# Gated one-hots with the tokens innermost, read with a step by TensorE, and one form for all bank copies

## The chip, the core and the metric

The kernel runs on one core of a Trainium2 chip. The metric is the device time of one execution in microseconds (us), lower is better. Times of a kernel are given as the median of several runs; one further execution is taken by the hardware profiler, and every row of the profile is of that one. Engines are named as in the profile: PE is TensorE's matrix product and PEld its weight load, DVE is VectorE, ACT is ScalarE, POOL is GpSimd, SP is SyncE, which issues most of the transfers.

## The reference

Two transformer blocks in float32 over 256 tokens of width 1024. The change lies in the last part of the second block, a layer of 16384 experts: each token picks, for each of 8 heads, 16 experts by two keys of 128, and each pick has a gate (a softmax over the 16).

```python
def peer_ffn(h, w_query, sub_keys, u_emb, v_emb):
    ...
        q = (hc @ w_query).reshape(B, T_CHUNK, PEER_HEADS, 2, PEER_DKEY // 2)
        s = jnp.einsum('bthpd,hpnd->bthpn', q, sub_keys).astype(jnp.float32)
        s_top, i_top = lax.top_k(s, PEER_TOPK)
        ...
        g_s, pos = lax.top_k(cand, PEER_TOPK)
        e_idx = jnp.take_along_axis(cand_idx, pos, axis=-1)
        g = jax.nn.softmax(g_s, axis=-1)
        u = u_emb[e_idx]
        act = jax.nn.gelu(jnp.einsum('btd,bthkd->bthk', hc, u).astype(jnp.float32), approximate=False)
        return jnp.einsum('bthk,bthkd->btd', (g * act).astype(h.dtype), v_emb[e_idx])
```

The kernel gathers nothing. It computes the activation of every token with every expert, multiplies it by a gate that is zero where the token has not picked the expert, and multiplies the product by all of `v`. For this it needs, for each token, a matrix of 128 x 128 gates: entry (p, i) is the gate of the expert with first key i and second key p.

## The kernel before

`peer` does the layer. It first routes: queries, scores, the top 16 of each head and their gates. Beside that, and long after it, runs a loop over 64 chunks of 256 experts. `first(c)` splits a chunk of `u` into two fp32r parts (ScalarE at L172 writes `hi`, VectorE at L173 writes `lo`), makes 48 matmuls into the tile `pa` (L179 to L181), and ScalarE takes the gelu at L1355. The activations of the first 48 chunks (`BANK`) go to memory and come back; `second(c)` multiplies a chunk by its gates (L1372) and by `v`.

While the chunks 19 to 47 are on TensorE, `gates` makes the 256 gate matrices in between: it is a generator, and the loop takes a step of it every now and then (`done < 33 * (c + 1 - START) // (BANK - START)`), so that on TensorE the products of one batch of 8 tokens stand between the matmuls of two chunks. A step first has `hots` make the next batch's one-hots on VectorE:

- L1293: `x`, tile `hot`, bf16, laid out [key, token] with the 8 tokens innermost: 1 where the token's slot has that first key. Slots are on the partitions.
- L1294: `y`, tile `m`, float32, laid out [token, key]: the same for the second key.
- L1295: `z`, tile `hotg`, float32, laid out [token, key]: `x` times the slot's gate. Here `x` is read across its layout, so that two elements read after each other lie 8 bf16 apart.

Then TensorE makes, for each token, one float32 product of `y` (stationary) and `z` (moving, 128 columns) at L1309, four tokens to a PSUM bank (tile `acc`, four buffers), and ScalarE copies each bank into the tile `k` (`out` in the code), whose layout is [key, token of 16]. The two banks of a batch are copied in different forms. The copy of the second bank, at L1313, walks key by key and writes four neighbouring floats at a time, reading PSUM 128 floats apart. That of the first, at L1315, walks token by token: it reads PSUM in a row and writes floats that lie 16 apart. After two batches SyncE writes the 16 tokens' gates to memory (L1317).

Buffers: `hot` has 2, `hotg` 3, the tile `m` of `y` 3, `acc` 4 and `pa` 2. Nothing is scheduled by a planner; each engine's queue keeps the order in which the code is written.

Of the kernel before, what the change touches and what calls it, by code (L numbers as in the profile page):

```python
# [11 lines left out]
BF16 = mybir.dt.bfloat16  # L12
# [3 lines left out]
OP = mybir.AluOpType  # L16
# [3 lines left out]
P = 128  # L20
# [50 lines left out]
class Net:  # L71
# [1199 lines left out]
    def gates(self, slots, iotas, gd):  # L1271


        nc = self.nc
        keys, gate = [], []
        for t in range(2):
            pt = self.ps([P, 3, P], "acc", 4)
            for i in range(3):
                nc.tensor.transpose(pt[:, i, :], slots[t][:, i, :, :].rearrange("p a b -> p (a b)"), self.ident)
            kt = self.work([P, P], "key0", 2, BF16), self.work([P, P], "key1", 2)  # L1280
            gt = self.work([P, P], "gate", 2)
            for z, i in ((kt[0], 0), (kt[1], 1), (gt, 2)):
                nc.scalar.copy(z, pt[:, i, :])
            keys.append(kt)
            gate.append(gt)
        n = 8
        made = {}

        def hots(b):
            t, o = divmod(n * b, P)  # L1290
            wide = lambda x: x[:, o : o + n].unsqueeze(2).to_broadcast([P, n, P])
            x, y, z = self.work([P, P, n], "hot", 2, BF16), self.m4([P, n, P]), self.work([P, n, P], "hotg", 3)
            nc.vector.tensor_tensor(x, iotas[1], keys[t][0][:, o : o + n].unsqueeze(1).to_broadcast([P, P, n]), op=OP.is_equal)  # L1293
            nc.vector.tensor_tensor(y, iotas[0].unsqueeze(1).to_broadcast([P, n, P]), wide(keys[t][1]), op=OP.is_equal)  # L1294
            nc.vector.tensor_tensor(z, x.rearrange("p k t -> p t k"), wide(gate[t]), op=OP.mult)  # L1295
            made[b] = y, z

        hots(0)
        yield
        for b in range(32):  # L1300
            if b < 31:
                hots(b + 1)
            if b % 2 == 0:
                out = self.keep([P, P, 16], "k8", 4)
            y, z = made.pop(b)
            for q in range(0, n, 4):
                pg = self.ps([P, 4, P], "acc", 4)
                for i in range(4):
                    nc.tensor.matmul(pg[:, i, :], y[:, q + i, :], z[:, q + i, :], start=True, stop=True)  # L1309
                r = n * (b % 2) + q  # L1310
                o = out[:, :, r : r + 4]
                if q:
                    nc.scalar.copy(o, pg.rearrange("p t i -> p i t"))  # L1313
                else:
                    nc.scalar.copy(o.rearrange("p i t -> p t i"), pg)  # L1315
            if b % 2:
                nc.sync.dma_start(gd[b // 2], out)  # L1317
            yield
# [245 lines left out]
```

## Time and profile before

| what | value |
|---|---|
| median of 3 runs (lowest to highest) | 1699.3 us (1696.49 to 1700.89) |
| the profiled execution, its time | 1695.26 us |
| its span, first to last instruction | 1693.5 us |
| TensorE busy, share of the span | 1624.9 us, 96% |
| VectorE busy | 1273.5 us, 75% |
| ScalarE busy | 833.6 us, 49% |
| mean granted TensorE clock | 0.986 of full speed |

The last of L1309's work is done near 1239 us; the gate matrices thus fill about an eighth of the span, from 1028 us on. Busy shares are means over the whole span: which engine sets the time in that eighth has to be read there. Durations of matmul records overlap, since matmuls are pipelined; how fast they follow one another is read from the chain, where each record has only the time that it adds.

### The profile page before, as it was taken

To read this page: it belongs to the slowest core of one execution; us is meant where nothing else is said; L and a number is where in the kernel's file an instruction comes from. 1 tells how busy PE (TensorE), PEld (TensorE's weight loads), DVE (VectorE), ACT (ScalarE), POOL (GpSimd) and SP (SyncE) were. 2 spreads that over 40 slices of the span, in tenths; PEclk is the share of its full clock that TensorE was granted. 3 is DMA by queue.
4 is the path that set the end of the run, shared out by engine and by line. 5 is a ranking of instruction groups with operands and counts; after the bars stand their busy time and mean duration, and the time that the engine had idled before them with its cause. 6 is when DMAs were issued, how large, how long until landed. Compare 5 with 4: busy or idle time off the path is not lost.

```text
span 1693.5 us, 27346 instructions
## 1 busy us (share of the span) xinstructions
PE 1624.9 (96%) x10518; PEld 1444.4 (85%) x10518; DVE 1273.5 (75%) x2042; ACT 833.6 (49%) x1229; POOL 168.8 (10%) x133
## 2 busy tenths in 40 slices
PE   7998999999968999999989999999999999999998
PEld 4875898988857988886789999999999998888886
DVE  7887688876966888947869888988845556776665
ACT  6546545442126455646644455555554444444444
POOL 0110100000001000000047770000000000000001
PEclk9999999999979999999999999999999999999999
DMA  9783499956415999474166666777786668999970
GB/s 376 267 286 125 147 345 344 339 178 221 139 38 206 365 330 349 164 263 149 59 230 203 216 210 231 275 250 252 255 285 218 211 214 281 336 315 324 320 252 34
DMA packets 145397, 406.63 MB, mean 240 GB/s; under 512 B 13169, under 2 KB 46065, under 8 KB 143090
## 3 DMA queue, kind: packets, MB, share of 16 engines
q1 hardware_dynamic: 137280, 390.66, 67.0%
q10 hardware_dynamic: 7474, 14.16, 2.2%
q8 instruction: 82, 1.34, 0.3%
q14 instruction: 49, 0.40, 0.1%
q0 software_dynamic: 512, 0.07, 0.0%
HBM read 374.43 MB, written 30.41 MB: 239 GB/s over the span
## 4 chain that ended last, share of the span: by engine, by line
PE 75%; issue 10%; DVE 3%; ACT 2%; DMA 1%; POOL 1%; SPq 0%; POOLq 0%; DVEq 0%; ACTq 0%
PE ps L179 7%; PE ps L181 7%; PE ps L180 7%; PE pa L179 7%; PE pa L181 7%; PE pa L180 7%; PE acc L180 7%; PE acc L181 7%; PE acc L179 7%; PE acc L1309 3%; PE ps L588 2%; PE ps L894 2%; DVE m L885 1%; DMA st<-w_ff 1%; PE ps L1171 1%
## 5 line engine op out<-in xcount | busy, mean ns | idle before, releaser
L172 ACT CAST hi<-st 128x1024 fp32r<-128x1024 f32 x466 | 474.3, 1046 | 444.7 <-PE pa L180 169.6
L173 DVE TENSOR_TENSOR lo<-st,hi 128x1024 fp32r<-128x1024 f32 (+1 forms) x416 | 495.5, 1219 | 176.2 <-ACT hi L172 170.7
L179 PE MATMUL pa<-k,hi 128*128 128x256 f32 x1024 | 289.4, 283 | 0.0
L180 PE MATMUL pa<-k,hi 128*128 128x256 f32 x1024 | 286.3, 280 | 0.0
L181 PE MATMUL pa<-k,lo 128*128 128x256 f32 x1024 | 286.3, 280 | 0.0
L179 PE MATMUL ps<-k,hi 128*128 128x256 f32 x816 | 230.0, 283 | 0.0
L180 PE MATMUL ps<-k,hi 128*128 128x256 f32 x816 | 229.4, 281 | 0.0
L181 PE MATMUL ps<-k,lo 128*128 128x256 f32 x816 | 229.4, 281 | 0.0
L179 PE MATMUL acc<-hi,m 128*128 128x512 f32 x512 | 199.7, 390 | 0.0
L180 PE MATMUL acc<-lo,m 128*128 128x512 f32 x512 | 199.3, 389 | 0.1
L181 PE MATMUL acc<-hi,m 128*128 128x512 f32 x512 | 199.3, 389 | 0.0
L180 PEld LDWEIGHTS pa<-k,hi 128*128 128x128 f32 x1024 | 194.1, 190 | 0.5
L181 PEld LDWEIGHTS pa<-k,lo 128*128 128x128 f32 x1024 | 193.4, 189 | 0.0
L179 PEld LDWEIGHTS pa<-k,hi 128*128 128x128 f32 x1024 | 192.3, 188 | 0.5
L179 PEld LDWEIGHTS ps<-k,hi 128*128 128x128 f32 x816 | 154.2, 189 | 3.4 <-issue 1.0
L181 PEld LDWEIGHTS ps<-k,lo 128*128 128x128 f32 x816 | 156.2, 191 | 0.6 <-DVE lo L173 0.5
L180 PEld LDWEIGHTS ps<-k,hi 128*128 128x128 f32 x816 | 154.9, 190 | 2.1 <-issue 0.5
L173 POOL TENSOR_TENSOR lo<-st,hi 128x1024 fp32r<-128x1024 f32 x50 | 119.0, 2406 | 35.4 <-ACT hi L172 26.1
L306 DVE SCALAR_TENSOR_TENSOR k<-st,sil,k 128x1024 f32<-128x1024 f32 x96 | 117.6, 1280 | 0.0
L181 PEld LDWEIGHTS acc<-hi,m 128*128 128x128 f32 x512 | 96.1, 188 | 20.3 <-DVE m L195 0.4
L180 PEld LDWEIGHTS acc<-lo,m 128*128 128x128 f32 x512 | 96.1, 188 | 20.1 <-DVE lo L173 0.5
L179 PEld LDWEIGHTS acc<-hi,m 128*128 128x128 f32 x512 | 96.1, 188 | 19.6 <-issue 0.2
(298 smaller groups left out, 2623.4 us busy)
## 6 DMA issues: line engine op xcount, KB each, us to landing
st<-w_ff SPq DMA_DIRECT2D x128, 512.0 KB, 6.1
st<-uT SPq DMA_DIRECT2D x128, 512.0 KB, 4.6
st<-v SPq DMA_DIRECT2D x128, 512.0 KB, 5.3
st<-w_mod SPq DMA_DIRECT2D x96, 512.0 KB, 5.9
st<-w_ada SPq DMA_DIRECT2D x48, 512.0 KB, 5.9
st<-w_in SPq DMA_DIRECT2D x44, 512.0 KB, 5.7
gates<-k SPq DMA_DIRECT2D x16, 1024.0 KB, 7.4
k<-gates SPq DMA_DIRECT2D x16, 1024.0 KB, 8.5
```

Source lines behind the costliest of these rows:

```text
L172: nc.scalar.copy(h, raw)
L173: self.last_lo = (lo or nc.vector).tensor_tensor(l, raw, h.bitcast(F32), op=OP.subtract)
L179: mm(ps, l.hi, r.hi, start=first, stop=False)
L180: mm(ps, l.hi, r.lo, start=False, stop=False)
L181: mm(ps, l.lo, r.hi, start=False, stop=last)
L306: nc.vector.scalar_tensor_tensor(t[:, s], st, by, t[:, s], op0=OP.mult, op1=OP.add)
L588: mm(p[:, j, :], wt[k][:, j * P : (j + 1) * P], h[:, k, :], start=k == 0, stop=k == KC - 1)
L885: nc.vector.scalar_tensor_tensor(v, z[:, i : i + T], self.col("w_dw", c * 31 + i), v, op0=OP.mult, op1=OP.add)
L894: nc.tensor.matmul(yt[t][c % 2][:, c // 2 * P : c // 2 * P + P], z[:, t * P + i : t * P + i + P], dg[:, i, :], start=i == 0, stop=False)
L1171: nc.tensor.matmul(po[64 * i : 64 * i + 64, c * P :], v[:, c, (hd - 1 + i) * 64 : (hd + i) * 64], pTs[hd - 1 + i][:, 2 * c : 2 + c, :], st ...
L1309: nc.tensor.matmul(pg[:, i, :], y[:, q + i, :], z[:, q + i, :], start=True, stop=True)
```

## The change

Two things change in `hots` and in the loop behind it. `z` gets the layout of `x`, [key, token] with the 8 tokens innermost. VectorE then reads `x` and writes `z` in one order, and reads the gates of 8 tokens in a row, repeated for each key. TensorE reads a token's 128 columns of `z` with a step of 8 floats. And the copy of the first bank takes the form that the second had, so that all 64 copies write four neighbouring floats at a time. The number of instructions on each engine and their order stay; only operands have another shape.

```diff
         def hots(b):
             t, o = divmod(n * b, P)
             wide = lambda x: x[:, o : o + n].unsqueeze(2).to_broadcast([P, n, P])
-            x, y, z = self.work([P, P, n], "hot", 2, BF16), self.m4([P, n, P]), self.work([P, n, P], "hotg", 3)
+            x, y, z = self.work([P, P, n], "hot", 2, BF16), self.m4([P, n, P]), self.work([P, P, n], "hotg", 3)
             nc.vector.tensor_tensor(x, iotas[1], keys[t][0][:, o : o + n].unsqueeze(1).to_broadcast([P, P, n]), op=OP.is_equal)
             nc.vector.tensor_tensor(y, iotas[0].unsqueeze(1).to_broadcast([P, n, P]), wide(keys[t][1]), op=OP.is_equal)
-            nc.vector.tensor_tensor(z, x.rearrange("p k t -> p t k"), wide(gate[t]), op=OP.mult)
+            nc.vector.tensor_tensor(z, x, gate[t][:, o : o + n].unsqueeze(1).to_broadcast([P, P, n]), op=OP.mult)
             made[b] = y, z
...
-                    nc.tensor.matmul(pg[:, i, :], y[:, q + i, :], z[:, q + i, :], start=True, stop=True)
+                    nc.tensor.matmul(pg[:, i, :], y[:, q + i, :], z[:, :, q + i], start=True, stop=True)
                 r = n * (b % 2) + q
                 o = out[:, :, r : r + 4]
-                if q:
-                    nc.scalar.copy(o, pg.rearrange("p t i -> p i t"))
-                else:
-                    nc.scalar.copy(o.rearrange("p i t -> p t i"), pg)
+                nc.scalar.copy(o, pg.rearrange("p t i -> p i t"))
```

## Rows read from the trace of the kernel before

**Rows 1.** The page: busy time by engine, and the span in 40 slices.

```profile
PE 1624.9 (96%) x10518; PEld 1444.4 (85%) x10518; DVE 1273.5 (75%) x2042; ACT 833.6 (49%) x1229; POOL 168.8 (10%) x133
...
PE   7998999999968999999989999999999999999998
```

**Rows 2.** Busy time by window while the gate matrices are made.

```profile
core 0: us, PE busy (x) PEld busy (x) DVE busy (x) ACT busy (x) POOL busy (x), PEclk, DMA share, GB/s
...
1028.00:1070.00 42.00, 42.00 (x370) 41.97 (x369) 41.93 (x37) 23.05 (x32) 0.00 (x0) 1.00 0.66 226
1070.00:1110.00 40.00, 40.00 (x351) 40.00 (x350) 37.21 (x32) 22.82 (x30) 0.00 (x0) 1.00 0.75 261
1110.00:1150.00 40.00, 40.00 (x352) 40.00 (x351) 35.91 (x30) 21.54 (x28) 0.00 (x0) 1.00 0.74 256
1150.00:1200.00 50.00, 50.00 (x438) 50.00 (x437) 43.49 (x37) 27.57 (x35) 0.00 (x0) 1.00 0.73 255
1200.00:1240.00 40.00, 40.00 (x352) 40.00 (x352) 27.03 (x21) 23.22 (x30) 1.51 (x2) 1.00 0.79 260
```

**Rows 3.** All waits of all engines from 1028 to 1241 us.

```profile
engine line waited for: us in total, times, longest us
POOL m L294 <- PE acc L1309: 215.3, 1, 215.3
ACT hi L172 <- PE pa L180: 93.6, 56, 3.5
DVE lo L173 <- ACT hi L172: 19.8, 25, 4.7
DVE lo L173 <- DMA st<-uT: 2.9, 3, 1.0
POOL m L296 <- POOL m L294: 0.3, 1, 0.3
```

**Rows 4.** The chain of work that ended last: start, microseconds, what.

```profile
1026.53 0.12 PE pa L179
1031.98 1.88 PE acc L1309 x16
1033.87 0.12 PE pa L179
1039.33 1.78 PE acc L1309 x16
...
1235.61 3.57 PE acc L1309 x32
1239.18 0.12 PE pa L179
```

**Rows 5.** Groups of instructions from 1028 to 1241 us, shapes apart.

```profile
line engine op names shapes xcount | busy us, mean ns | idle before us <-releasers
L179 PE MATMUL pa<-k,hi 128*128 128x256 f32 x450 | 127.7, 284 | 0.0
...
L1295 DVE TENSOR_TENSOR hotg<-hot,gate 128x1024 f32<-128x1024 bf16 x32 | 64.1, 2005 | 0.0
L1309 PE MATMUL acc<-hotg,m 128*128 128x128 f32 x512 | 61.8, 275 | 0.0
...
L172 ACT CAST hi<-st 128x1024 fp32r<-128x1024 f32 x56 | 58.8, 1050 | 93.6 <-PE pa L180 93.6
L1294 DVE TENSOR_TENSOR m<-iota,key 128x1024 f32<-128x1024 f32 x32 | 39.0, 1220 | 0.0
L1315 ACT COPY k<-acc 128x512 f32<-128x512 f32 x32 | 34.4, 1076 | 0.0
L1293 DVE TENSOR_TENSOR hot<-iota,key 128x1024 bf16<-128x1024 bf16 x32 | 21.7, 689 | 0.6
L1313 ACT COPY k<-acc 128x512 f32<-128x512 f32 x32 | 20.7, 647 | 0.0
L1355 ACT ACTIVATE act<-pa 128x512 f32<-128x512 f32 x28 | 16.6, 592 | 0.0
```

**Rows 6.** Groups of the whole span: other widths of float32 products, a VectorE operation.

```profile
L588 PE MATMUL ps<-k,st 128*128 128x256 f32 x192 | 42.6, 379 | 0.0
...
L328 PE MATMUL ps<-k,ones 128*128 128x512 f32 x16 | 7.5, 592 | 0.0
...
L1235 DVE TENSOR_TENSOR m<-acc,sm 128x256 f32<-128x256 f32 x16 | 6.5, 406 | 0.0
```

**Rows 7.** One window, from 1241 us to the end.

```profile
1241.00:1694.00 453.00, 444.96 (x2341) 382.91 (x2339) 284.05 (x306) 208.68 (x251) 5.00 (x5) 0.99 0.76 253
```

## The prediction

> **What bounds the kernel now.** I read the page's busy times and slices first, then the stretch in which the changed lines run. TensorE is busy for 96% of the span, and in slices 25 to 29, where the gate matrices are made, its digit is 9 [rows 1]. The windows say it sharper: in each of the five windows from 1028 to 1240 us TensorE is busy the whole time at a granted clock of 1.00 (the 2.4 GHz level), while VectorE fills 41.93 us of the first 42 and then less and less, and ScalarE a little over half [rows 2]. A busy TensorE need not be at its peak, so I read the waits and the chain too. In the waits between 1028 and 1241 us nothing on TensorE waits for anybody: ScalarE and VectorE wait for TensorE and for each other [rows 3]. The chain of work that ended last consists in this stretch of TensorE alone: 16 records of L1309, then the 48 matmuls of one expert chunk, then 16 records of L1309 again, end to end [rows 4]. So here a microsecond on TensorE is a microsecond of the kernel, and one on VectorE or ScalarE is not.
>
> **The stepped read by TensorE.** The 256 gate products stay 256, and each is seen as two records, 512 in all [rows 5]. At the end of the stretch 32 records take 3.57 us [rows 4], so one follows another after 3.57 / 32 = 111.6 ns, and all 512 take 57.1 us of the chain. What a column costs comes from the float32 matmuls of three widths: 592 ns for 512 columns, 379 for 256, 275 for 128 [rows 5, 6]. (592 - 379) / 256 = 0.83 ns a column; 128 of them are 106.5 ns, and 5.1 ns of the 111.6 are left over for each record. After the change the 128 moving columns lie 8 floats, 32 bytes, apart instead of 4 bytes.
>
> No matmul of the trace reads its moving operand with such a step, so its cost is bounded by the two nearest rows, both on other engines.
> - VectorE, reading: L1295 reads its one-hots 8 bf16, 16 bytes, apart. It takes 2005 ns for 1024 elements, where L1294 takes 1220 for as many without that step [rows 5]. The step costs 785 / 1024 = 0.77 ns an element. Without it an element costs (1220 - 406) / 768 = 1.06 ns, from L1294 and the 256-element L1235 [rows 5, 6]; with it 1.83.
> - ScalarE, writing: the copy at L1315 writes 16 floats apart and takes 1076 ns for 512 elements, the one at L1313 writes four together and takes 647 [rows 5]. That is 0.84 ns more an element. A plain element costs (1050 - 592) / 512 = 0.89 ns, from L172 and L1355 [rows 5]; with the step 1.73.
>
> Two engines with different paces of their own (1.06 and 0.89 ns) thus end at nearly the same time for an element that lies alone: 1.83 and 1.73 ns. That looks like a limit of the memory rather than of either engine, and TensorE, at 0.83 ns a column, asks for twice what it allows. If it holds for TensorE, a record takes 128 x 1.73 + 5.1 = 226.5 ns or, by the VectorE row, 128 x 1.83 + 5.1 = 239.3 ns. Against 111.6 that is 114.9 or 127.7 ns more, times 512: **58.8 or 65.4 us**. The other bound is zero: a stepped column that costs no more than 0.83 ns is hidden by the float32 pace itself. Less than zero is excluded, as the same 128 columns are multiplied at the same pace. I take 58.8, the ScalarE row: its elements have four bytes, as TensorE's have, and its plain pace is the nearest to 0.83.
>
> The weight loads are untouched: y keeps its layout, and they lie under the matmuls as before.
>
> A rule to weigh here: the Trainium skill, page "Advanced Engine Details and Errata", section "SBUF Cachelines", says that SBUF has lines of 16 bytes, that an access to the same line as the one before runs at full speed, and that a line must be hit at least twice for its latency to be hidden. This trace agrees for VectorE and ScalarE (2005 against 1220 ns, 1076 against 647 ns). The page has no price and doesn't say at which pace of the reader the rule begins to bite, so the sum by it is only "above zero".
>
> **The multiplication on VectorE.** L1295 loses its stepped read: x and z now have one layout, and the gate is read 8 in a row and repeated over the keys, as L1293 reads its keys already. It should take what L1294 takes, 1220 ns with float32 output [rows 5], so 32 x 785 ns = 25 us less on VectorE. What this is worth is zero: TensorE waits for nobody in the stretch [rows 3], and the one-hots of a batch are made a batch ahead. Should it stay at 2005 ns, the time doesn't change either.
>
> **The bank copies on ScalarE.** 32 copies go from 1076 to 647 ns: 13.7 us less [rows 5]. No order moves; there are 64 copies as before. Worth zero for the same reason: ScalarE idles 93.6 us of the stretch, waiting for TensorE's chunks [rows 3], and no TensorE instruction waits for a bank. If instead the form with the stepped PSUM read got slower when every copy has it, 32 x 0.43 us would still lie in that idle time.
>
> **What is late next.** With TensorE slower, the chunks that follow, the bank copies and the writing of the gates shift by the same amount, and VectorE and ScalarE idle longer. Nothing catches up: from 1241 us to the end TensorE is busy 444.96 of 453 us [rows 7].
>
> **Sum.** The profiled execution took 1695.3 us (a span of 1693.5 and 1.8 around it); with 58.8 it would be 1754.1. It lies 4.0 us below the median of the three runs, 1699.3; I put the same 58.8 on the median: 1758.1. By the VectorE row it is 1764.7. A measurement here can tell a change of 0.3%, about 5 us, from none.
>
> **Rivals.**
> - *The float32 pace hides the step: no change, 1699.* The place is the same, the 512 records. The price is zero if TensorE needs a column only every 0.83 ns and gets a stepped one in that time; that is the point from which it decides. For it: the neighbouring matmuls in fp32r show that TensorE's read path can be faster than float32 needs, for 256 columns take 284 ns there against 379 in float32 [rows 5, 6]. If a step merely halves that faster rate, it stays hidden. Against it: two engines that want elements at 0.89 and 1.06 ns don't get lone ones at that pace. Chance 0.36. By a rule of the Trainium skill, page "TensorE: Matmul & The Clock Gate", Part 2 (step FILL), the throughput of a matmul is purely its number of columns, whatever their place; no row of this trace has a stepped moving operand to show it.
> - *A column is fetched twice.* Float32 takes twice the time of fp32r a column; if each of the two steps fetched a lone element at 1.73 ns, a record would take 128 x 3.46 + 5.1 = 448 ns, 336 more, times 512: 172 us, about 1871. Only the pace itself speaks for it. 0.04.
> - *Something between.* A lone element at 1.0 to 1.6 ns gives 11 to 50 us: 1710 to 1749. Against it: no row shows such a price. 0.06.
> - *VectorE was the bound after all: faster.* It is full in the first 42 us [rows 2], and 25 us of its work go. But TensorE shows no wait. Even in the rest of the kernel TensorE isn't busy for only 453.0 - 445.0 = 8 us [rows 7], so at best it is 1691. 0.04.
>
> **How the numbers follow.** The forecast, a lone column at 1.7 to 1.85 ns, has 0.50: 1753 to 1767, with 1758 as the time. The range has to take in the no-change rival (0.36) and what lies between (0.06), so it runs from 1694 to 1768 and leaves out the double fetch, a little of the faster case and some of the forecast's own upper edge. Faster 0.04, same 0.36, slower 0.50 + 0.04 + 0.06 = 0.60.
>
> **What would show it.** In the profile of the changed kernel L1309 should still have 512 records, 16 of them taking about 3.6 us on the chain instead of 1.78, with mean durations near 390 ns instead of 275; the stretch from the first to the last of them should be longer by nearly the whole difference of the spans. L1295 should stand at about 1220 ns and all 64 bank copies at about 647. VectorE's and ScalarE's busy time should fall by about 25 and 14 us without any gain. The prediction is wrong if L1309 keeps 111.6 ns a record (no change), or if TensorE begins to wait for VectorE, ScalarE or a transfer in this stretch.

## The result and the profile after

The changed kernel takes 1761.8 us (median of 3, 1758.3 to 1766.1) against 1699.3: ratio 1.039, 95% interval 1.036 to 1.042. It is slower by 62.5 us, where 58.8 were forecast. The profiled execution took 1761.8 us with a span of 1760.0, 66.5 more than before.

The page of the changed kernel, busy time by engine, beside [rows 1]:

```profile
span 1760.0 us, 27346 instructions
...
PE 1692.8 (96%) x10518; PEld 1497.7 (85%) x10518; DVE 1252.3 (71%) x2042; ACT 826.2 (47%) x1229; POOL 169.0 (10%) x133
```

TensorE gained 67.9 us of work at the same number of instructions; VectorE lost 21.2 and ScalarE 7.4. The shares hardly say so: 96% stays 96%.

The chain of work that ended last, start and microseconds, beside [rows 4]:

```profile
1033.81 3.73 PE acc L1309 x16
...
1043.19 3.73 PE acc L1309 x16
...
1298.45 7.46 PE acc L1309 x32
```

A batch of 16 records takes 3.73 us where it took 1.78. A record follows the one before after 7.46 / 32 = 233.1 ns instead of 111.6, and 512 x 121.5 ns = 62.2 us. From the start of the first batch to the end of the last it is 272.1 us (1305.91 - 1033.81) after 207.2 (1239.18 - 1031.98): 64.9 more, 62.2 of them these records. The other 2.7 lie in the expert chunks between: from one batch to the next they take some 5.65 us each, where about every second one took 5.46 before; no run shows why. The rest of the kernel is as long as before: the last batch ended 454.3 us before the end of the span, and now ends 454.1 us before it. The granted clock is 1.00 throughout the stretch, as before [rows 2], so a slower clock is not what doubles the records:

```profile
core 0: us, PE busy (x) PEld busy (x) DVE busy (x) ACT busy (x) POOL busy (x), PEclk, DMA share, GB/s
1028.00:1070.00 42.00, 42.00 (x298) 40.40 (x297) 32.86 (x33) 17.48 (x29) 0.00 (x0) 1.00 0.61 209
...
1250.00:1300.00 50.00, 50.00 (x341) 47.82 (x341) 24.86 (x22) 21.43 (x28) 1.51 (x2) 1.00 0.54 195
```

Groups of instructions in the stretch from 1028 to 1310 us of the changed kernel, beside [rows 5]:

```profile
line engine op names shapes xcount | busy us, mean ns | idle before us <-releasers
...
L1309 PE MATMUL acc<-hotg,m 128*128 128x128 f32 x512 | 123.8, 411 | 0.0
...
L1294 DVE TENSOR_TENSOR m<-iota,key 128x1024 f32<-128x1024 f32 x32 | 39.2, 1225 | 41.6 <-PE acc L1309 41.6
L1295 DVE TENSOR_TENSOR hotg<-hot,gate 128x1024 f32<-128x1024 bf16 x32 | 39.0, 1219 | 0.0
L1312 ACT COPY k<-acc 128x512 f32<-128x512 f32 x64 | 37.5, 586 | 58.3 <-PE acc L1309 58.3
```

The multiplication on VectorE fell from 2005 to 1219 ns, the copies to 586, as the change intends. What is new is the idle time: VectorE waits 41.6 us and ScalarE 58.3 us for the gate products. Before, neither engine waited for L1309 [rows 3, 5]. The engines that were relieved wait for the one that was slowed.

### The profile page after: what moved, and what is told of

The parts are those of the page before. It is cut to its first block, busy times and chain, and to the rows that moved or that the text cites. A ratio compares the mean times of both kernels' runs of the same rounds, so it can differ in the third digit from the quotient of the medians.

```text
span 1760.0 us, 27346 instructions
## 1 busy us (share of the span) xinstructions
PE 1692.8 (96%) x10518; PEld 1497.7 (85%) x10518; DVE 1252.3 (71%) x2042; ACT 826.2 (47%) x1229; POOL 169.0 (10%) x133
## 4 chain that ended last, share of the span: by engine, by line
PE 76%; issue 10%; DVE 3%; ACT 2%; DMA 1%; POOL 1%; SPq 0%; POOLq 0%; DVEq 0%; ACTq 0%
PE ps L179 7%; PE ps L181 7%; PE ps L180 7%; PE pa L180 7%; PE pa L179 7%; PE pa L181 7%; PE acc L1309 7%; PE acc L180 6%; PE acc L181 6%; PE acc L179 6%; PE ps L588 2%; PE ps L894 1%; DVE m L885 1%; PE ps L575 1%; PE ps L1171 1%
## 5 line engine op out<-in xcount | busy, mean ns | idle before, releaser
L173 DVE TENSOR_TENSOR lo<-st,hi 128x1024 fp32r<-128x1024 f32 (+1 forms) x416 | 496.3, 1219 | 225.2 <-ACT hi L172 223.4
L1309 PE MATMUL acc<-hotg,m 128*128 128x128 f32 x512 | 123.8, 411 | 0.0
L173 POOL TENSOR_TENSOR lo<-st,hi 128x1024 fp32r<-128x1024 f32 x50 | 119.0, 2405 | 35.4 <-ACT hi L172 31.7
L181 PEld LDWEIGHTS acc<-hi,m 128*128 128x128 f32 x512 | 96.1, 188 | 20.3 <-DVE m L195 0.4
```

What stands on the lines that cost most here:

```text
L173: self.last_lo = (lo or nc.vector).tensor_tensor(l, raw, h.bitcast(F32), op=OP.subtract)
L181: mm(ps, l.lo, r.hi, start=False, stop=last)
L1309: nc.tensor.matmul(pg[:, i, :], y[:, q + i, :], z[:, :, q + i], start=True, stop=True)
```

## The experiments

Three theories stood against each other at first. L: an element alone in its 16 bytes costs a fixed time, whoever reads it; this is the prediction's reason. H: a step halves the pace at which the moving operand streams. B: only certain steps collide. A fourth, C, puts the loss on the copies. Records are timed on the chain. The kernels ran on several chips; before took 1690.7 to 1696.7 us on these (medians, on two of them a single run).

**The two parts apart.** First the change without its last hunk, the copies as before. 

> Only the layout of z changes, TensorE reads with a step of 32 bytes; the two copy forms stay as before. Theory L (lone elements: an element that shares its 16 bytes with no other element of the read costs about 1.78 ns, whoever reads it): the records of L1309 follow one another after 233 ns instead of 111.6, 512 x 121.5 ns = 62 us more than before. Theory C (the copies: 64 copies that all read PSUM with a step hold up TensorE's writes to PSUM): most of the 62 us are gone, records near 112 to 150 ns.

Second the last hunk alone:

```diff
-                if q:
-                    nc.scalar.copy(o, pg.rearrange("p t i -> p i t"))
-                else:
-                    nc.scalar.copy(o.rearrange("p i t -> p t i"), pg)
+                nc.scalar.copy(o, pg.rearrange("p t i -> p i t"))
```

> Only the copies change, z stays as before. Theory L: no change of time (within 5 us), records at 111.6 ns, ScalarE's copies 32 x 0.43 = 13.7 us cheaper. Theory C: records above 112 ns and up to 62 us more.

The layout alone: 1761.8 us against 1696.7, ratio 1.038 (1.035 to 1.040). The copies alone: 1698.2, ratio 1.001 (0.998 to 1.003). The chain of the layout alone:

```profile
1300.20 7.46 PE acc L1309 x32
```

and, of the kernel with the copies alone, the chain and the copies' group in the stretch from 1028 to 1310 us:

```profile
1239.01 3.57 PE acc L1309 x32
```

```profile
L1312 ACT COPY k<-acc 128x512 f32<-128x512 f32 x64 | 35.3, 583 | 2.3 <-PE acc L1309 2.3
```

So the whole loss is the stepped read, and the cheaper copies are worth nothing that can be measured. C falls.

**Shorter and odder steps.** z in groups of 2 tokens (8 bytes between columns), of 4 (16 bytes), of 2 in three floats (12 bytes), and 8 tokens in nine floats (36 bytes). The edit for pairs, with parts of long lines; the others accordingly (for 36 bytes z is `[P, P, n + 1]`):

```diff
-self.work([P, P, n], "hotg", 3)
+self.work([P, n // 2, P, 2], "hotg", 3)
...
-            nc.vector.tensor_tensor(z, x, gate[t][:, o : o + n].unsqueeze(1).to_broadcast([P, P, n]), op=OP.mult)
+            for u in range(n // 2):
+                nc.vector.tensor_tensor(z[:, u, :, :2], x[:, :, 2 * u : 2 * u + 2],
+                                        gate[t][:, o + 2 * u : o + 2 * u + 2].unsqueeze(1).to_broadcast([P, P, 2]), op=OP.mult)
...
-z[:, :, q + i], start=True
+z[:, (q + i) // 2, :, (q + i) % 2], start=True
```

> As after, but z laid out in pairs of tokens, so that TensorE's step is 2 floats, 8 bytes (the product z is made by 4 smaller instructions). Theory L: two columns share 16 bytes, 1.78 / 2 = 0.89 ns a column, 128 x 0.89 + 5.1 = 119 ns a record, 3.8 us more than before. Theory H (any step halves the pace of the moving operand): 233 ns a record, 62 us more than before. Theory B (a conflict that only a step of 32 bytes or a multiple has): 111.6 ns, nothing more than before.

> As after, but z laid out in fours of tokens: TensorE's step is 4 floats, 16 bytes (z made by 2 instructions). Theory L: every column alone in its 16 bytes, 233 ns a record, 62 us more than before, no less than at 32 bytes. Theory H: 233 ns too. Theory B: clearly less than 233 ns, down to 111.6.

> As the kernel with pairs of tokens, but each pair in three floats, so that TensorE's step is 12 bytes (one buffer of z less, for room). With 8 bytes a record took 113.4 ns, with 16 bytes 226.6, with 32 bytes 233.1. Theory L, a cost for each 16-byte line that the read touches, 226.6 / 128 = 1.77 ns: 128 columns at 12 bytes touch 96 lines, 96 x 1.77 = 170 ns a record, 512 x 58 = 30 us more than before. Theory H (from a step of 16 bytes on, the pace is halved; below it is whole): 112 to 114 ns, no change.

> As after, but with a ninth float behind each 8 tokens that nothing uses, so that TensorE's step is 36 bytes, no power of two. Theory L: still a line of its own for each column, 227 to 233 ns a record, 60 to 62 us more than before. Theory B (what costs is that steps of 16 and 32 bytes meet in the same part of the memory): clearly less than 226 ns.

The last line of the gate products in the chain of each: 8 bytes, 16, 12, 36.

```profile
1241.54 3.63 PE acc L1311 x32
```

```profile
1286.25 7.25 PE acc L1311 x32
```

```profile
1256.87 5.49 PE acc L1311 x32
```

```profile
1294.73 7.39 PE acc L1309 x32
```

Divided by 32 that is 113.4, 226.6, 171.6 and 230.9 ns a record. The kernels took 1700.2 us (ratio 1.002, 1.001 to 1.004) and, in one run each, 1748.6, 1719.5 and 1757.4. B falls: neither the shorter 16 bytes nor the uneven 36 are clearly cheaper than 32 (226.6 and 230.9 against 233.1 ns). H, for every step or for those from 16 bytes on, falls in float32 with the 8 and the 12 bytes: the one is almost free, and the other lies between, where a cost per 16 bytes touched puts it (96 of them in 128 columns; 96 x 1.77 = 170 ns). At 16 bytes, 226.6 / 128 = 1.77 ns a column. The Trainium skill, page "Advanced Engine Details and Errata", section "SBUF Cachelines", names the 16-byte lines; the float32 products agree with that size.

**Is the time the memory's or the reader's?** With y and z as fp32r, the four-byte type of the kernel's expert chunks, each product is one record at the fast pace. L and H now differ by a factor of two. The edit, with parts of long lines:

```diff
-x, y, z = self.work([P, P, n], "hot", 2, BF16), self.m4([P, n, P]), self.work([P, P, n], "hotg", 3)
+x, y, z = self.work([P, P, n], "hot", 2, BF16), self.m4([P, n, P], F32R), self.work([P, P, n], "hotg", 3, F32R)
```

> As after (step of 32 bytes), but y and z are fp32r, so that each of the 256 products is one record at the fast pace; the gates are rounded to fp32r. Theory L: the lines set the pace, not the engine: 128 x 1.82 = 233 ns a record, 256 x 233 = 59.7 us on the chain in place of before's 57.1, so 2.5 us more than before. Theory H (a wide step halves the engine's own pace): about 2 x 57 = 114 ns, 29 us on the chain, 28 us less than before.

> The layouts of before with y and z as fp32r and all copies in one form; the gates are rounded to fp32r. TensorE reads without a step. Theory L: 128 columns are 32 lines, 57 ns of reading, about 57 to 60 ns a record, 256 of them 15 us in place of 57.1: up to 42 us less than before, less where VectorE, which is full in the first 42 us of before, cannot keep up (it needs 32 x 3.9 + 57 x 1.22 = 195 us for the stretch, where TensorE would need 175): then some 20 us less. Theory H expects the same.

The chain of the fp32r kernel with a step, and of the one without:

```profile
1072.03 1.77 PE acc L1309 x16
...
1203.73 0.88 PE acc L1309 x8
```

```profile
1052.03 0.84 PE acc L1309 x8
```

1.77 / 16 = 110.6 ns a record with the step, where L wanted 233. A lone column is had in 110.6 / 128 = 0.86 ns. **L falls, and with it the reason that the prediction gave.** Without a step it is 0.84 / 8 = 105 ns, not the 57 to 60 I expected: with 128 columns something else than the read sets the pace. So the next two take 256 columns for each stationary operand; the edit for 32 bytes, the other likewise with z in pairs:

```diff
-                for i in range(4):
-                    nc.tensor.matmul(pg[:, i, :], y[:, q + i, :], z[:, :, q + i], start=True, stop=True)
+                for i in range(0, 4, 2):
+                    nc.tensor.matmul(pg[:, i : i + 2, :], y[:, q + i, :], z[:, :, q + i : q + i + 2].rearrange("p k t -> p t k"), start=True, stop=True)
```

> As the fp32r kernel with a step of 32 bytes, but each matmul takes two tokens, 256 moving columns, for one stationary operand, so that no weight load can hide the read (the odd tokens are multiplied by the wrong one-hots). 128 records. Without a step 256 fp32r columns take 114 to 118 ns. Theory P: twice that, 221 to 233 ns a record, 0.86 to 0.91 ns a column. Theory L (a line costs 1.77 ns whoever reads it): 453 ns.

> The same 256 columns in fp32r with a step of 8 bytes, z in pairs of tokens (the odd tokens are multiplied by the wrong one-hots). Theory P: two columns share a line, so the step is free: 114 to 118 ns a record. Theory L: 128 lines x 1.77 = 227 ns. Theory H (any step halves the pace in fp32r): 221 to 233 ns.

Chains, 32 bytes and then 8:

```profile
1070.10 1.75 PE acc L1309 x8
```

```profile
1064.55 1.81 PE acc L1311 x8
```

218.8 and 226.3 ns for 256 columns, 0.85 and 0.88 ns each. Theory P, which I had put in L's place (two column slots for each line), said 114 to 118 for 8 bytes and falls too: in fp32r even the step of 8 bytes, free in float32, doubles the time.

**All steps in one kernel.** To see both modes side by side I gave 16 cases a source line each.

```diff
+                flat, mm = z.rearrange("p k t -> p (k t)"), nc.tensor.matmul
+                step = lambda s: flat[:, : P * s].rearrange("p (k s) -> p s k", s=s)
...
+                if b // 2 == 3:
+                    [mm(pg[:, i : i + 2, :], y[:, q + i, :], step(4)[:, 0:2, :], start=True, stop=True) for i in (0, 2)]
...
+                if b // 2 == 11:
+                    [mm(pg[:, i, :], y[:, q + i, :].bitcast(F32), step(4)[:, 0, :].bitcast(F32), start=True, stop=True) for i in range(4)]
```

> One kernel with sixteen cases on lines of their own, two batches each: 256 fp32r columns and 128 float32 columns at steps of 1 to 8 floats, all from one buffer of z whatever its layout (so the gate values are wrong, and only the pace of the records is read). Theory L (1.77 ns for each 16-byte line touched): fp32r records of 256 columns take 114, 227, 340 and then 453 ns from 16 bytes on, float32 ones of 128 columns 112, 113, 170 and then 227 to 233. Theory Q (in fp32r any step costs one price, some 0.85 to 0.89 ns a column, and only float32 goes by lines): fp32r 114 and then 219 to 227 at every step from 8 to 32 bytes; float32 as in L.

Its chain; L1311 to L1325 are fp32r with 256 columns at steps of 1 to 8 floats, L1327 to L1341 float32 with 128 columns at the same steps:

```profile
1037.96 0.47 PE acc L1311 x4
1043.89 0.91 PE acc L1313 x4
...
1056.63 0.92 PE acc L1315 x4
...
1069.60 1.86 PE acc L1317 x8
1076.91 0.92 PE acc L1319 x4
...
1089.86 0.91 PE acc L1321 x4
...
1102.78 0.88 PE acc L1323 x4
...
1115.46 1.74 PE acc L1325 x8
1122.67 1.78 PE acc L1327 x16
...
1137.35 1.82 PE acc L1329 x16
...
1152.29 2.77 PE acc L1331 x16
...
1169.14 7.25 PE acc L1333 x32
1181.85 3.68 PE acc L1335 x16
...
1200.52 3.62 PE acc L1337 x16
...
1219.09 3.70 PE acc L1339 x16
...
1237.60 7.46 PE acc L1341 x32
```

Divided by the records and the columns, in ns a column:

| step, bytes | 4 | 8 | 12 | 16 | 20 | 24 | 28 | 32 |
|---|---|---|---|---|---|---|---|---|
| fp32r | 0.46 | 0.89 | 0.90 | 0.91 | 0.90 | 0.89 | 0.86 | 0.85 |
| float32 | 0.87 | 0.89 | 1.35 | 1.77 | 1.80 | 1.77 | 1.81 | 1.82 |

This is theory Q, with small misses in the size (fp32r records with a step take 217 to 233 ns where it said 219 to 227): about one price in fp32r as soon as there is a step, some twice the plain one; in float32 a price that grows up to 16 bytes and then nearly stays, twice the plain one too. Each case was run once, over two batches.

**The step on the other operand.** y and z change places in the call.

```diff
-nc.tensor.matmul(pg[:, i, :], y[:, q + i, :], z[:, :, q + i], start=True, stop=True)
+nc.tensor.matmul(pg[:, i, :], z[:, :, q + i], y[:, q + i, :], start=True, stop=True)
```

> As after, but the operands change places: z with its step of 32 bytes is the stationary one, y without a step the moving one (this gives each gate matrix transposed). Theory P (a read that touches a new 16-byte line with each element costs two of the reader's own column slots): the moving operand is at full pace again, but the weight load, one column in 105 / 128 = 0.82 ns, is doubled to some 210 ns a record, so 45 to 60 us more than before. Theory W (weight loads are pulled ahead of the matmuls and don't show): 111.6 ns a record, as before.

1761.8 us in one run; a line of its chain:

```profile
1090.64 7.61 PE acc L1309 x32
```

237.8 ns a record, as slow as the stepped moving operand. W falls: the stepped weight load is not hidden here. P's 210 was too low.

## Why the prediction was right, and where it was not

- *The place and the sign held.* The range from 1694 to 1768 took in the no-change rival too, so it is the point, 1758 against 1761.8, that tells something. (By the prediction's own sum, 1.7 to 1.85 ns a column give 1756 to 1766, not 1753 to 1767.) TensorE alone sets the time in the stretch [rows 3, 4]; 62.2 of the 66.5 us between the two spans stand on L1309, and the layout alone gives the same loss as the whole change.
- *The size held, with the term a little low.* 114.9 ns more a record were forecast from the ScalarE row and 127.7 from the VectorE row; measured are 121.5. The 6.6 ns that the ScalarE row is low are as much as the step of 32 bytes costs over that of 16 (233.1 against 226.6), for which no run shows a reason.
- *The reason behind that term failed.* The step that says lone elements look like "a limit of the memory rather than of either engine" is refuted: the fp32r products take lone columns at 0.85 to 0.91 ns, half of the 1.73 to 1.83 that the two other engines' rows gave. What holds on TensorE is that a stepped column costs about twice what the same mode costs without a step (fp32r 0.85 to 0.91 against 0.46, float32 from 16 bytes on 1.77 to 1.82 against 0.87). That float32 doubled then meets the prices of ScalarE and VectorE follows from nothing that these runs show, and the number came out right through that luck. Had the gate products been in fp32r, the same argument would have forecast 226.5 ns a record where 110.6 were measured.
- *The 5.1 ns left over for each record* are neither shown nor refuted beside the stepped read. All stepped float32 records here have 128 columns, so a price for each column and a rest for each record cannot be told apart: 226.6 ns at 16 bytes are 128 x 1.77, but also 128 x 1.73 + 5.1.
- *The rival "the float32 pace hides the step"* is wrong at 32 bytes and right at 8 (113.4 ns a record; the kernel takes 3.5 us more, 0.9 of them on these records). "Something between" is what 12 bytes give. Of the double fetch, the price of 1.73 ns for each of two fetches is refuted; two fetches of a lone element at some 0.9 ns would give the float32 price at 16 bytes and more, but then 8 bytes should not be free, so I leave the mechanism inside TensorE's read open.
- *VectorE and ScalarE.* 32 x 786 ns = 25.1 us came off L1295, as forecast, and bought nothing. ScalarE's copies went from 34.4 + 20.7 = 55.1 to 37.5 us, 17.6 less instead of 13.7, because the 647 ns row was not the price of that copy (below). The stepped write's price of 1.73 ns hardly suffers from it: in the kernel with the layout alone, where both forms wait for TensorE, the rows are 1022 and 586 ns, 0.85 instead of 0.84 ns more an element. The page's busy times fell by less, 21.2 and 7.4 us, since durations of neighbours that overlap count once there. The rival that VectorE is the bound falls with the first kernel of the experiments: there VectorE is relieved too, and the time goes up.
- By the rule of the Trainium skill, page "TensorE: Matmul & The Clock Gate", Part 2, that a matmul's throughput is purely its number of columns, nothing should have changed; float32 from 12 bytes on and fp32r from 8 show the opposite (1.35 ns and more against 0.87, 0.85 and more against 0.46). The two hits on a 16-byte line that the Trainium skill, page "Advanced Engine Details and Errata", section "SBUF Cachelines", asks for are enough in float32 (8 bytes: 0.89 against 0.87 ns), but not in fp32r, where 8 bytes leave two columns to a line and still cost double.

**A kernel that beats both.** With fp32r gate products the layout of the change becomes usable: 1666.8 us against 1693.3 of before, ratio 0.983 (0.979 to 0.987); the gates are rounded to fp32r in it. 256 records at 110.6 ns are 28.3 us on the chain instead of 57.1, 28.8 less, and the medians differ by 26.5. The same products without a step, VectorE paying 2006 ns for z, gave 0.987 (0.984 to 0.991); the two intervals overlap, so which layout is better in fp32r is not settled. Of the 30.2 us that its 105 ns a record would give, that kernel has 20.6. Some of the rest lies on VectorE: from 1057 to 1086 us its chain runs over L1293 to L1295 and L173, and not over TensorE; how much that makes was not worked out.

## What to carry to other kernels

Where TensorE sets the time, moving a layout's step from VectorE onto a matmul operand can double that matmul. It did so in float32 with 128 columns from 16 bytes between them on, and on the stationary operand too (tried at 32 bytes); in fp32r with 256 columns it did so from 8 bytes on, while with 128 columns 32 bytes cost only 5% (110.6 against 105 ns). In float32 two columns side by side in 16 bytes were enough to have the read nearly free. A price taken from another engine's row is good for a bound; before trusting the reason behind it, ask for a second mode or size in which the theories differ.

## What was not expected of the hardware

- Plain fp32r products show a price like the stepped ones in bytes: records of 512 columns follow one another after 227 ns in both kernels (in the lines below 12 of them take 2.72 us), 0.443 ns a column or 1.77 ns for 16 bytes, the same 1.77 ns that float32 needs for a column alone in its 16. Whether the plain fp32r products of this kernel, most of its work, are held by that read and not by the multiplier was not tried. From the chain of before:

```profile
1258.64 0.23 PE acc L179
...
1261.36 0.23 PE acc L179
```

- A row can contain its neighbour. The copy with four floats together stood at 647 ns in [rows 5], behind another copy; with all 64 in that form it takes 583, and 586 where it waits for TensorE. In before's timeline (start, duration) the second copy starts before the first has ended:

```profile
1101.22 1.09 ACT L1315 COPY k<-acc 128x512 f32<-128x512 f32 x1
...
1102.08 0.66 ACT L1313 COPY k<-acc 128x512 f32<-128x512 f32 x1
```

- 128 plain fp32r columns take 105 ns a record and 256 take 117: at 128 columns another cost than the read sets the pace, and a step is nearly hidden under it (110.6). Which cost that is, and from how many columns on the read is the slower one, was not tried.
